# A hybrid decoder layer: the recurrent stage's small products in one run per unit, its distances by ScalarE's bias, the samples' heads gated together

## The chip, the cores and the metric

The kernel is one program on one core of a Trainium2 chip. The metric is device time of one execution in microseconds (us). Before the change three runs took 2379.52, 2382.35 and 2384.54 us, a median of 2382.35 us.

## The reference

One inference step of a hybrid layer for a prompt of 2048 tokens and for 8 samples of 4 tokens: a norm, one input projection, sparse attention (compressed, selected and window keys), a gated linear recurrence with 4 heads, a gated merge of both, an output projection, a last norm. The change is in the recurrence and in when attention's bias tables are loaded. Per head the recurrence is this (`gc` is the log of the forget gate, at most zero):

```python
def step(S, xs):                      # one chunk; S is 128 x 128 per head
    qc, kc, vc, gc = xs
    G = jnp.cumsum(gc, axis=2)
    o_inter = einsum('bhtd,bhde->bhte', qc * exp(G), S)
    D = where(tri, G[:, :, :, None, :] - G[:, :, None, :, :], -inf)
    A = einsum('bhtd,bhtsd,bhsd->bhts', qc, exp(D), kc)
    o = o_inter + einsum('bhts,bhse->bhte', A, vc)
    Gl = G[:, :, -1, :]
    S = exp(Gl)[..., None] * S + einsum('bhsd,bhse->bhde', kc * exp(Gl[:, :, None, :] - G), vc)
    return S, o
...
o = o * rsqrt(mean(o * o, axis=-1, keepdims=True) + EPS)
return o.reshape(B, T, B_WIDTH) * norm_g * silu(zB), S
```

The decay `exp(D)` differs per key channel, so `A` isn't one matrix product.

## The kernel before

The program is written as generators that yield to one another. A projection generator feeds TensorE with 512-column products (line 375, `ps`, weights `wh`/`wl`, inputs `xh`/`xl`). It runs beside the compression of keys, then beside `hgrn()`, the recurrent stage, and then prompt attention follows with the merge. Each `yield` of `hgrn()` grants the projection some 1200 ns worth of products, so these stand between the recurrent steps in TensorE's queue. A framework derives buffers, waits and each engine's order of instructions; every engine takes its queue in that order, and a wait holds what is behind it on the same engine.

`hgrn()` treats 32 units, 8 chunks of 256 tokens by 4 heads. A unit has two halves of 128 tokens (index `j`). Its steps:

- `common()` loads `lf` (log gate), `kt` and `qt`, scans the running sum `G` on VectorE, and makes `Bq`, `Bk` (distances inside groups of 4 tokens), `Xo` (query times `exp(G)`) and `Kd` (key times the decay to the end of the half: a subtraction `E2` on VectorE, line 704, an exponential on ScalarE, a product on GpSimd).
- `factors()` splits the decay between two tokens at the middle of the smallest block that holds both. For each of five levels (64, 32, 16, 8, 4) it makes a tile `X` of `exp(-|G - G at the block's middle|)`: the distance on VectorE (line 732), Abs and Exp on ScalarE (733, 734), keys and queries multiplied in by GpSimd (735, 736). Factors are made two units ahead.
- `scores()` transposes `Kd` (line 743) and multiplies the factors. Each half has a PSUM tile `p4` of its own. Line 755 makes the level-64 product (64 x 64) and two level-32 products (32 x 32); line 759 makes the near ones: levels 16, 8, 4 and `Bk`/`Bq`, each at four diagonal positions of 32 rows and 32 columns of the array. ScalarE copies the far blocks into the score tile `AT` (762, 764). VectorE picks from the four near levels by masks: one product and three `copy_predicated` into `own`, and one into `AT` (766 to 769).
- `values()` makes the state's update (778), the outputs from scores and state (782, 784), the new state (789) and the squares for the norm. After four heads the inverse root follows by three Newton steps (241 to 244), then scale, gate and two stores per head (`gate_scale`, `gate_out`, 658 to 672).
- `sample_heads()` does the samples' 32 tokens, one head at a time, from the seventh unit on, with operands of 32 rows or 32 columns (817, 822, 824, 829, 839, 846), and a norm, a gate and two stores for each head.

The stage starts with its own loads (masks, then `lf`, `kt`, `qt` of the first unit). Ahead of them in the queue of SP, the engine that issues the loads and stores, stand twelve Toeplitz loads of the bias tables (lines 1354 and 1356: `th`, `tl`, `tq`), which prompt attention uses later. Behind the stage, `load_keys` (lines 1397 to 1401) loads the selected keys and values in two parts, t0 = 0 and t0 = 512, while the merge's projection writes its rows by pieces (line 441).

Of the kernel before, what the change touches and what calls it, by code (L numbers as in the profile page):

```python
# [10 lines left out]
F32 = mybir.dt.float32  # L11
# [120 lines left out]
def trunk_kernel(ctx: ExitStack, tc: tile.TileContext, A, O):  # L132
# [100 lines left out]
    def newton_rsqrt(ss, pool):  # L233
# [386 lines left out]
    def hgrn():  # L620
        with ExitStack() as st:
# [6 lines left out]
            lmi = hc.tile([128, 8, 32], I32, name="lmi")  # L628
            ve.tensor_copy(lmi, lm)
            lm3 = hc.tile([128, 32], F32, name="lm3")  # L630
            ve.tensor_copy(lm3, lm[:, 3])
# [17 lines left out]
            def rsqrt(ss):  # L649
                n = ss.shape[0]  # L650
                ve.tensor_scalar(ss, ss, 1.0 / 128, EPS, op0=OP.mult, op1=OP.add)
                y = hp.tile([128, 8], F32, name="rsy", bufs=3)[:n, :ss.shape[1]]
                ve.tensor_scalar(y, newton_rsqrt(ss, hp), sob[:n], None, op0=OP.mult)
                return y

            def gate_scale(o_sb, y, nt, r):

                ve.tensor_tensor(o_sb[:r, :nt], o_sb[:r, :nt], y[:r, :nt, None].to_broadcast([r, nt, 128]), op=OP.mult)

            def gate_out(o_sb, zt, nt, r, h, t0):  # L660
                pt = po.tile([128, 512], F32, name="ov")
                for j in range(nt):
                    pe.transpose(pt[:, j * 128:j * 128 + r], o_sb[:r, j], ident[:r, :r])
                n = (nt - 1) * 128 + r
# [6 lines left out]
                sy.dma_start(obh_d[h * 128:(h + 1) * 128, t0:t0 + n], gh[:, :n])  # L671
                sy.dma_start(obl_d[h * 128:(h + 1) * 128, t0:t0 + n], gl[:, :n])

            def common(h, t0, n, L):
# [3 lines left out]
                def new(name, bufs=2):  # L678
                    return hp.tile([128, n], F32, name=name + sfx, bufs=bufs if n == NC or name == "E" else 1)

                lf = new("lf")
                kt = new("kt", bufs=2)
                qt = new("qt", bufs=2)
# [35 lines left out]
            def factors(c, h):  # L719
# [5 lines left out]
                for li, L in enumerate(LEVELS):  # L725
# [6 lines left out]
                    ve.tensor_tensor(Xv, Gv, ref, op=OP.subtract)  # L732
                    ac.activation(X, X, AF.Abs)
# [6 lines left out]
            def scores(u):  # L740
# [4 lines left out]
                ac.activation(u["kd"], pk[:, :NJ], AF.Copy)  # L745
                u["AT"] = []
                for j in range(NJ):
                    tj = slice(j * 128, (j + 1) * 128)
                    p4 = pa.tile([128, 4, 128], F32, name="p4")

                    near = p4[:, 1].rearrange("p (l t) -> p l t", l=4)
                    for li, L in enumerate(LEVELS[:2]):
                        X = u["Xs"][li][:, tj]
                        for s0 in range(0, 128, 2 * L):
                            mm(p4[s0:s0 + L, 0, s0 + L:s0 + 2 * L], X[:, s0:s0 + L], X[:, s0 + L:s0 + 2 * L], li == 0 or s0 == 64, True)
                    for li, (l, r) in enumerate([(x, x) for x in u["Xs"][2:]] + [(u["Bk"], u["Bq"])]):
                        for b in range(4):
                            bs = slice(j * 128 + 32 * b, j * 128 + 32 * b + 32)
                            mm(near[32 * b:32 * b + 32, li], l[:, bs], r[:, bs], li == 0 and b == 3, True)
# [1323 lines left out]
```

## Time and profile before

| | us |
|---|---|
| median of 3 runs | 2382.35 (2379.52 to 2384.54) |
| profiled execution, its own time | 2394.12 |
| its span (mean granted clock 0.982) | 2392.4 |
| TensorE (PE) busy | 2276.5, 95% |
| VectorE (DVE) busy | 1523.3, 64% |
| ScalarE (ACT) busy | 1180.8, 49% |
| GpSimd (POOL) busy | 1018.8, 43% |

PEld is TensorE's loading of weights, beside its products. A row of a timeline names start, length, engine, line, operation, tiles and count; neighbours of one kind and line are drawn together into one row, so that a row's length covers all of its instructions, and a product's end is modelled: the start of the next is the surer mark. Idle time is put down to the instruction that released the engine, or to "issue" where the profile shows nothing that it waited for. A row by stretch counts busy time of each engine within the two times given.

### The profile page before, as it was taken

To read this page: it belongs to the slowest core of one execution; us is meant where nothing else is said; L and a number is where in the kernel's file an instruction comes from. 1 tells how busy PE (TensorE), PEld (TensorE's weight loads), DVE (VectorE), ACT (ScalarE), POOL (GpSimd) and SP (SyncE) were. 2 spreads that over 40 slices of the span, in tenths; PEclk is the share of its full clock that TensorE was granted. 3 is DMA by queue.
4 is the path that set the end of the run, shared out by engine and by line. 5 is a ranking of instruction groups with operands and counts; after the bars stand their busy time and mean duration, and the time that the engine had idled before them with its cause. 6 is when DMAs were issued, how large, how long until landed. Compare 5 with 4: busy or idle time off the path is not lost.

```text
span 2392.4 us, 56947 instructions
## 1 busy us (share of the span) xinstructions
PE 2276.5 (95%) x22181; PEld 1543.9 (65%) x22181; DVE 1523.3 (64%) x4089; ACT 1180.8 (49%) x2606; POOL 1018.8 (43%) x1184
## 2 busy tenths in 40 slices
PE   6999998999899999999999999899999999999998
PEld 4888775555586556566665556567667666665765
DVE  7555554756632599888753466777677676767543
ACT  5544331531332266666642266356556566667563
POOL 0000102332430065566620045266556576768764
PEclk9999999999999999999999999999999999999999
DMA  6543312677762333443324433322222221211121
GB/s 201 171 142 116 130 72 88 228 250 245 234 161 72 136 133 117 143 128 104 123 87 139 126 113 111 102 62 84 75 77 86 59 69 55 59 47 50 51 59 42
DMA packets 276111, 271.91 MB, mean 114 GB/s; under 512 B 102296, under 2 KB 246176, under 8 KB 268416
## 3 DMA queue, kind: packets, MB, share of 16 engines
q1 hardware_dynamic: 267328, 230.51, 31.5%
q0 software_dynamic: 8512, 37.75, 4.8%
q8 instruction: 174, 2.85, 0.5%
q14 instruction: 97, 0.79, 0.1%
HBM read 184.66 MB, written 87.74 MB: 114 GB/s over the span
## 4 chain that ended last, share of the span: by engine, by line
PE 75%; DVE 9%; DMA 6%; ACT 3%; issue 3%; SPq 2%; POOL 1%; another core or an unknown queue 0%; DVEq 0%; POOLq 0%; ACTq 0%
PE ps L375 19%; PE ps L1847 7%; PE ps L1815 7%; PE ps L456 6%; PE ps L435 5%; PE st L1704 3%; PE st L1694 3%; PE mx L1570 3%; PE ph L1005 2%; PE po L1495 2%; PE po L1498 2%; PE po L1496 2%; PE pt L988 1%; DMA wraw<-in_w_in_dram 1%; PE mx L1572 1%
## 5 line engine op out<-in xcount | busy, mean ns | idle before, releaser
L1489 POOL TENSOR_TENSOR Pl<-P,Ph 128x512 f16<-128x512 f32 x444 | 522.0, 1185 | 355.6 <-ACT Ph L1488 234.6
L1487 ACT ACTIVATE P<-st 128x512 f32<-128x512 f32 x444 | 264.9, 597 | 253.6 <-PE st L1704 199.5
L375 PEld LDWEIGHTS <-wh 128*128 128x128 f16 x2240 | 214.9, 99 | 164.4 <-issue 16.1
L1488 ACT ACTIVATE Ph<-st 128x512 f16<-128x512 f32 x444 | 263.4, 595 | 18.4 <-PE po L1496 11.7
L375 PE MATMUL ps<-xh,wh 128*128 128x512 f16 (+1 forms) x1120 | 234.4, 344 | 6.2 <-DVE row L388 3.5
L375 PE MATMUL ps<-xh,wl 128*128 128x512 f16 (+1 forms) x1120 | 235.3, 345 | 0.0
L375 PE MATMUL ps<-xl,wh 128*128 128x512 f16 (+1 forms) x1120 | 231.8, 342 | 1.2 <-issue 1.2
L1573 DVE TENSOR_REDUCE mps<-mx 128x1 f32<-128x512 f32 (+3 forms) x320 | 186.3, 602 | 55.3 <-PE mx L1570 31.7
L456 PE MATMUL ps<-wh,xh 128*128 128x256 f16 (+1 forms) x680 | 190.9, 281 | 12.3 <-ACT to L464 7.2
L456 PE MATMUL ps<-wh,xl 128*128 128x256 f16 (+1 forms) x680 | 189.9, 280 | 3.9 <-DVE xl L341 3.9
L456 PE MATMUL ps<-wl,xh 128*128 128x256 f16 (+1 forms) x680 | 190.3, 280 | 0.0
L375 PEld LDWEIGHTS <-wl 128*128 128x128 f16 x1120 | 110.2, 100 | 81.1 <-issue 4.4
L1495 PEld LDWEIGHTS <-Ph 128*128 128x128 f16 x1776 | 140.0, 98 | 34.3 <-DVE otmp L1587 3.8
L456 PEld LDWEIGHTS <-xh 128*128 128x128 f16 x1360 | 131.7, 100 | 34.8 <-issue 9.6
L1496 PEld LDWEIGHTS <-Ph 128*128 128x128 f16 x1776 | 128.8, 97 | 32.8 <-issue 0.7
L735 POOL TENSOR_TENSOR X<-X,kt 128x128 f32<-128x128 f32 x160 | 90.6, 566 | 115.2 <-ACT X L734 110.4
L1573 DVE TENSOR_REDUCE mpw<-mx 128x1 f32<-128x512 f32 (+3 forms) x224 | 103.0, 483 | 45.7 <-PE mx L1572 44.0
L1815 PEld LDWEIGHTS <-xh 128*128 128x128 f16 x1280 | 104.5, 98 | 31.6 <-issue 7.8
L1498 PEld LDWEIGHTS <-Pl 128*128 128x128 f16 x1776 | 94.3, 97 | 25.6 <-POOL Pl L1489 7.1
L1495 PE MATMUL po<-vs,Ph 128*128 128x65 f16 x1088 | 105.5, 192 | 2.1 <-DVE otmp L1587 2.0
L1847 PE MATMUL ps<-xh,yh 128*128 128x512 f16 (+1 forms) x272 | 103.0, 379 | 2.3 <-DVE pr L1818 2.3
L1496 PE MATMUL po<-vs,Ph 128*128 128x64 f16 x1088 | 105.1, 193 | 0.0
(529 smaller groups left out, 5740.7 us busy)
## 6 DMA issues: line engine op xcount, KB each, us to landing
wraw<-in_w_in_dram SPq DMA_DIRECT2D x22, 1024.0 KB
xt<-in_x_prompt_dram SPq DMA_DIRECT2D x32, 512.0 KB
ma_d<-row SPq DMA_DIRECT2D x8, 1040.0 KB
out_y_prompt_dram<-xt SPq DMA_DIRECT2D x16, 512.0 KB
sg<-ma_d SPq DMA_DIRECT2D x56, 128.0 KB
sg<-mb_d SPq DMA_DIRECT2D x56, 128.0 KB
q_d<-row SPq DMA_DIRECT2D x4, 1040.0 KB
lf_d<-row SPq DMA_DIRECT2D x4, 1040.0 KB
```

Of the source, the lines that this page charges most:

```text
L375: mm(ps, l[:, kc], xs(r, t0, n)[:, kc], k == 0, k == 23)
L435: mm(ps, l[:, kc, a * 128:(a + 1) * 128], xs(r, t0, n)[:, kc], k == 0, k == 23)
L456: mm(ps, x, w[:, kc], k == 0, k == 23)
L1487: ac.activation(P[:n], ps, AF.Exp, scale=1.0 / QS)
L1488: ac.activation(ph[:n], ps, AF.Exp, scale=1.0 / QS)
L1489: sub.tensor_sub(pl[:n], P[:n], ph[:n])
L1495: mm(po[:, r, :w], ph[:n, rs[r]], v[:n, :w], first and r == 0, False)
L1496: mm(po[:, r, :64], ph[:n, rs[r]], v[:n, w:w + 64], False, False)
L1498: mm(po[:, r, :w], pl[:n, rs[r]], v[:n, :w], False, last)
L1573: ve.tensor_reduce(mp_[:, r, c:c + 1], pmf[:, :n], axis=AX.X, op=OP.max)
L1815: mm(X["ps"], w[:, kc, cs], os_[o][:, kc], k == 0, k == 11)
L1847: mm(X["ps"], X["y"][y][:, kc, i0:i0 + r], W["o", kc // 4][w][:, kc % 4, cs], k == 0, k == 23)
```

## The change

- `newton_rsqrt` becomes `near_rsqrt`: two steps of a higher order in place of three, with the constants folded into the last product.
- The near levels are picked by one product with four 0/1 masks and a sum over the levels, in place of a product and three `copy_predicated`.
- `Kd` and the level-64 distance take no subtraction on VectorE: ScalarE computes `exp(bias - G)` and `|bias - G|` with a per-partition bias, in two calls of 128 columns each.
- The products of a unit go into one `p4` tile for both halves, in one piece of code at raised priority. All use 32 columns of the array: the level-64 product is two products of 32 columns, each with 64 columns moving. The first are those of level 4 (`X4`), then `Bk`/`Bq`.
- `lf`, `kt` and `qt` have three buffers. At the start three more yields stand between the factors of the first and of the second unit.
- The samples' operands are padded with zeros to 128 rows and columns. The outputs of the four heads are collected in `oT`, and there is one transpose, norm, gate and pair of stores for all of them, at the end.
- The Toeplitz loads move to `load_keys`: the four `tq` ahead of the first part, the eight `th`/`tl` behind the second part's keys and ahead of its values.

The diff, cut to its core:

```diff
-        for _ in range(3):
-            ve.tensor_mul(z, y, y)
+        for c in (1.0, 9.0 / 64):
+            ve.scalar_tensor_tensor(z, y, c, y, op0=OP.mult, op1=OP.mult)
             ve.tensor_mul(z, z, ss)
-            ve.tensor_scalar(z, z, -0.5, 1.5, op0=OP.mult, op1=OP.add)
-            ve.tensor_mul(y, y, z)
+            ve.scalar_tensor_tensor(z, z, -10.0 / 3, z, op0=OP.add, op1=OP.mult)
+            ve.scalar_tensor_tensor(y, z, 5.0, y, op0=OP.add, op1=OP.mult)
...
-                lf = new("lf")
-                kt = new("kt", bufs=2)
-                qt = new("qt", bufs=2)
+                lf = new("lf", bufs=3)
+                kt = new("kt", bufs=3)
+                qt = new("qt", bufs=3)
...
-                E2 = new("E", bufs=2)
-                ve.tensor_tensor(E2.rearrange("p (b i) -> p b i", i=L), GL[:, :, L - 1:L].to_broadcast([128, n // L, L]), GL, op=OP.subtract)
                 Kd = new("Kd")
-                ac.activation(Kd, E2, AF.Exp)
+                if n == NC:
+                    for b in range(n // L):
+                        ac.activation(Kd[:, b * L:(b + 1) * L], GL[:, b], AF.Exp, scale=-1.0, bias=GL[:, b, L - 1:L])
...
-                    ve.tensor_tensor(Xv, Gv, ref, op=OP.subtract)
-                    ac.activation(X, X, AF.Abs)
+                    if nb == 2:
+                        for b in range(2):
+                            ac.activation(Xv[:, b], Gv[:, b], AF.Abs, scale=-1.0, bias=Gv[:, b, L - 1:L])
+                    else:
+                        ve.tensor_tensor(Xv, Gv, ref, op=OP.subtract)
+                        ac.activation(X, X, AF.Abs)
...
+                p4 = pa.tile([128, 4, 128], F32, name="p4")
+                first = set()
+                for j in range(NJ):
+                    prod = []
+                    for li, (l, r) in reversed(list(enumerate([(x, x) for x in u["Xs"][2:]] + [(u["Bk"], u["Bq"])]))):
+                        for b in range(4):
+                            bs = slice(j * 128 + 32 * b, j * 128 + 32 * b + 32)
+                            prod.append((b, p4[32 * b:32 * b + 32, 2 * j + 1, 32 * li:32 * li + 32], l[:, bs], r[:, bs]))
+                    prod = prod[4:8] + prod[:4] + prod[8:]
+                    for li, L in enumerate(LEVELS[:2]):
+                        X = u["Xs"][li][:, j * 128:(j + 1) * 128]
+                        for s0 in range(0, 128, 2 * L):
+                            for c0 in range(s0, s0 + L, 32):
+                                prod.append((c0 // 32, p4[c0:c0 + 32, 2 * j, s0 + L:s0 + 2 * L], X[:, c0:c0 + 32], X[:, s0 + L:s0 + 2 * L]))
+                    with tc.high_priority():
+                        for b, o, l, r in prod:
+                            mm(o, l, r, b not in first, True)
+                            first.add(b)
...
-                    ve.tensor_mul(own, near[:, 3], lm3)
-                    for li in range(3):
-                        ve.copy_predicated(own, lmi[:, li], near[:, li])
-                    ve.copy_predicated(AT, lmi[:, 4:], own[:, None, :].to_broadcast([128, 4, 32]))
+                    each = hp.tile([128, 4, 32], F32, name="each")
+                    ve.tensor_mul(each, near, lm4)
+                    ve.tensor_reduce(own, each.rearrange("p l t -> p t l"), axis=AX.X, op=OP.add)
+                    ve.copy_predicated(AT, lmi, own[:, None, :].to_broadcast([128, 4, 32]))
...
-                        for b in range(4):
-                            ve.tensor_scalar(vm[:, b], v, bd[:, 4 * b2 + b:4 * b2 + b + 1], None, op0=OP.mult)
+                        ve.tensor_tensor(vm_[:32], v[:, None].to_broadcast([32, 4, 128]), bd[:, 4 * b2:4 * b2 + 4, None].to_broadcast([32, 4, 128]), op=OP.mult)
...
-                    mm(pb[:32, :32], Bk, Bq, True, True)
+                    mm(pb[:, :32], WIDE["Bk"], Bq, True, True)
...
-                    mm(ov, v, AT, True, False)
+                    mm(ov, v_, AT_, True, False)
...
-                    gate_out(o_sb, load_z(h, 2048, 32), 1, 32, h, 2048)
...
+                pe.transpose(pt[:, :128], oT.rearrange("p h t -> p (h t)"), ident)
...
+                gate_out(o_sb, zt, 1, place)
...
-            for _ in range(3):
+            for _ in range(6):
                 yield
...
+                for g in range(2):
+                    for dl in range(2):
+                        a["TB"][g, dl] = [pc_.tile([128, 4, 128], F16, name=f"t{hl}{g}{dl}") for hl in "hl"]
+                        tq = a["TQ"][g, dl] = pc_.tile([128, 4, 128], F16, name=f"tq{g}{dl}")
+                        sy.dma_start(tq, a["toep"](brh_d, g * 4 * 2 * BRN + BRN + (BRN - 1 - BR0) - 127 - 128 * dl, [[1, 128], [2 * BRN, 4], [1, 128]]))
                 sy.dma_start(a["sel0"], A["c_sel0"].rearrange("p (t j) -> p t j", j=32))
...
+            if t0 > 0:
+                for (g, dl), ts_ in a["TB"].items():
+                    for t_, br in zip(ts_, (brh_d, brl_d)):
+                        sy.dma_start(t_, a["toep"](br, g * 4 * 2 * BRN + BR0 + 128 * dl - 127, [[1, 128], [2 * BRN, 4], [1, 128]]))
```

In TensorE's order before, one half of a unit late in the stage stands like this, behind the transposes of its `Kd` (the size at a row's end is that of the output, with its count; `vs_`, `ATs`, `S0` belong to the samples):

```order
L743 MATMUL pk_14206<-ident_60,Kd_13932 128x128 x2
L755 MATMUL p4_14211<-X0_13939 64x64
L755 MATMUL p4_14211<-X1_13945 32x32 x2
L759 MATMUL p4_14211<-X2_13951 32x32
L822 MATMUL pu_14114<-ATs_13902,vs__13891 128x32
L824 MATMUL pu_14114<-Xo_s_13881,S0_13893 128x4 x8
L759 MATMUL p4_14211<-X2_13951 32x32 x3
L759 MATMUL p4_14211<-X3_13957 32x32 x4
L759 MATMUL p4_14211<-X4_13963 32x32 x4
L759 MATMUL p4_14211<-Bq_13921,Bk_13922 32x32 x4
L375 LDWEIGHTS wh_12587
```

The sample's value product and its eight state products stand in the middle of the half, and projection products (line 375) follow at once. Over the whole program the products of lines 755 and 759 stand in 121 such runs; 2760 projection products of line 375 stand ahead of the first.

After the change the same unit stands in one piece, behind a transpose of another unit's gate (line 663):

```order
L663 MATMUL ov_13843<-ident_60,o_sb_12985 128x128
L777 MATMUL p4_14196<-X4_13969 32x32 x4
L777 MATMUL p4_14196<-Bq_13928,Bk_13929 32x32 x4
L777 MATMUL p4_14196<-X3_13963 32x32 x4
L777 MATMUL p4_14196<-X2_13957 32x32 x4
L777 MATMUL p4_14196<-X0_13945 32x64 x2
L777 MATMUL p4_14196<-X1_13951 32x32 x2
L777 MATMUL p4_14196<-X4_13969 32x32 x4
```

The last row is the first of the second half, whose six rows follow with nothing between them; then come the next gate's transpose and a sample's (`Kd_s`). Over the program these products (line 777) stand in 32 runs, and 2613 projection products are ahead of the first.

In SP's queue before, where attention opens, the second part of the keys (`kas`, `kbs`) and the second part of the values (`vs16`) follow one another, between two writes of projection rows (`mb_d`):

```order
L1401 DMA vs16_16495<-vsx_d_93 128x4x258
L441 DMA mb_d_76<-piece_16538 128x512
L1397 DMA kas0_16491<-ksx_d0_89 64x1536
L1398 DMA kbs0_16492<-ksx_d0_89 128x1536
L1397 DMA kas1_16493<-ksx_d1_90 64x1536
L1398 DMA kbs1_16494<-ksx_d1_90 128x1536
L1401 DMA vs16_16495<-vsx_d_93 128x12x258
L1988 DMA szt_17834<-sz_d_69 128x2x128
L1988 DMA szt_18007<-sz_d_69 128x2x128
L1516 DMA kx1_19305<-kwx_d1_92 128x256
L441 DMA mb_d_76<-piece_16600 128x512
```

The twelve Toeplitz loads stand far ahead of this, in one block before the loads of the recurrent stage. After the change eight of them are at this place:

```order
L1433 DMA kas1_16237<-ksx_d1_90 64x1536
L1434 DMA kbs1_16238<-ksx_d1_90 128x1536
L1440 DMA th00_16240<-brh_d_85 128x4x128
L1440 DMA tl00_16241<-brl_d_86 128x4x128
L1440 DMA th01_16244<-brh_d_85 128x4x128
L1440 DMA tl01_16245<-brl_d_86 128x4x128
L1440 DMA th10_16248<-brh_d_85 128x4x128
L1440 DMA tl10_16249<-brl_d_86 128x4x128
L1440 DMA th11_16252<-brh_d_85 128x4x128
L1440 DMA tl11_16253<-brl_d_86 128x4x128
L1441 DMA vs16_16239<-vsx_d_93 128x12x258
L441 DMA mb_d_76<-piece_16560 128x272
```

They stand behind the keys and ahead of the values and of the next writes of rows. The other four, `tq`, stand ahead of the keys' first part.

## Rows read from the trace of the kernel before

**Rows 1.** The page: busy time by engine, and the chain that ended last.
```profile
PE 2276.5 (95%) x22181; PEld 1543.9 (65%) x22181; DVE 1523.3 (64%) x4089; ACT 1180.8 (49%) x2606; POOL 1018.8 (43%) x1184
...
PE 75%; DVE 9%; DMA 6%; ACT 3%; issue 3%; SPq 2%; POOL 1%; another core or an unknown queue 0%; DVEq 0%; POOLq 0%; ACTq 0%
```

**Rows 2.** By stretch: length, busy us (x instructions) by engine, clock, DMA share, GB/s.
```profile
606.00:720.00 114.00, 102.25 (x949) 81.20 (x948) 56.97 (x122) 45.85 (x114) 43.11 (x60) 0.97 0.71 200
...
836.00:1240.00 404.00, 386.98 (x4187) 245.59 (x4186) 333.13 (x1019) 249.66 (x888) 238.16 (x392) 0.97 0.38 122
...
1300.00:1330.00 30.00, 28.65 (x210) 18.05 (x209) 8.89 (x34) 6.94 (x12) 2.31 (x2) 1.00 0.85 226
```

**Rows 3.** TensorE in order of time: start, us, engine, line, operation, out<-in.
```profile
1043.10 0.48 PE L755 MATMUL p<-X 128*64 128x64 f32 x4
1043.38 0.23 PE L759 MATMUL p<-X 128*32 128x32 f32 x2
...
1043.43 0.34 PE L759 MATMUL p<-X 128*32 128x32 f32 x20
...
1043.63 0.26 PE L759 MATMUL p<-Bq,Bk 128*32 128x32 f32 x7
1043.82 0.61 PE L375 MATMUL ps<-xh,wh 128*128 128x512 f16 x2
...
1048.16 1.46 PE L375 MATMUL ps<-xh,wh 128*128 128x512 f16 x6
1049.55 0.25 PE L817 MATMUL pk<-Bq_s,Bk_s 128*32 128x32 f32 x2
1049.73 0.60 PE L375 MATMUL ps<-xh,wh 128*128 128x512 f16 x2
1050.17 1.89 PE L375 MATMUL ps<-xl,wh 128*128 128x512 f16 x8
1051.90 0.59 PE L375 MATMUL ps<-xh,wl 128*128 128x512 f16 x2
1052.42 0.48 PE L755 MATMUL p<-X 128*64 128x64 f32 x4
...
1052.93 0.44 PE L743 MATMUL pk<-ident,Kd 128*128 128x128 f32 x2
1053.29 0.35 PE L759 MATMUL p<-X 128*32 128x32 f32 x18
...
1053.67 1.47 PE L375 MATMUL ps<-xh,wl 128*128 128x512 f16 x6
```

**Rows 4.** The products' tile: idle time of the engine before them, us, times.
```profile
  issue: 26.2, 85
...
  POOL X L736: 9.4, 6
```

**Rows 5.** Groups of instructions, 606 to 1240: busy us, mean ns, idle before.
```profile
L759 PE MATMUL p<-X 128*32 128x32 f32 x1536 | 38.3, 201 | 0.0
L755 PE MATMUL p<-X 128*32 128x32 f32 (+1 forms) x384 | 35.1, 222 | 4.5 <-POOL X L736 3.4 <-DVE own L768 1.2
...
L759 PE MATMUL p<-Bq,Bk 128*32 128x32 f32 x512 | 20.5, 201 | 0.0
```

**Rows 6.** The same by shape: two of VectorE, two of ScalarE.
```profile
L732 DVE TENSOR_TENSOR X<-G 128x256 f32<-128x256 f32 x160 | 72.2, 494 | 14.0 <-PE p L759 8.3 <-PE p L755 3.7 <-POOL X L736 1.4
...
L394 ACT ACTIVATE row<-ps,neg 128x512 f32<-128x512 f32 x48 | 32.8, 683 | 65.5 <-PE ps L375 65.3
...
L704 DVE TENSOR_TENSOR E<-G 128x256 f32<-128x256 f32 x32 | 18.5, 578 | 0.2
...
L797 ACT ACTIVATE jk<-ov 128x128 bf16<-128x128 f32 x60 | 16.5, 275 | 0.2
```

**Rows 7.** The page, a call of ScalarE with constant scale and bias.
```profile
L1487 ACT ACTIVATE P<-st 128x512 f32<-128x512 f32 x444 | 264.9, 597 | 253.6 <-PE st L1704 199.5
```

**Rows 8.** One line of Toeplitz loads: ns of an issue, min/median/max.
```profile
L1356 SPq DMA_DIRECT2D tq<-brh_d x4: 506/508/702, 607.8 to 614.3; - x4
```

More of the change, by code (lines that the diff above doesn't have):

```diff
@@ L627, in hgrn @@
             sy.dma_start(lm, A["c_lmask"].rearrange("p (l t) -> p l t", l=8))
[L628 to L631, printed above, removed]
+            lmi = hc.tile([128, 4, 32], I32, name="lmi")
+            ve.tensor_copy(lmi, lm[:, 4:])
+            lm4 = hc.tile([128, 4, 32], F32, name="lm4")
+            ve.tensor_copy(lm4, lm[:, :4])
             ATs = []
@@ L670, in gate_out @@
                 ve.tensor_sub(gl[:, :n], g[:, :n], gh[:, :n])
-                sy.dma_start(obh_d[h * 128:(h + 1) * 128, t0:t0 + n], gh[:, :n])
-                sy.dma_start(obl_d[h * 128:(h + 1) * 128, t0:t0 + n], gl[:, :n])
+                for d, x in ((obh_d, gh), (obl_d, gl)):
+                    to, x = place(d, x)
+                    sy.dma_start(to, x)
+            WIDE = {}
             def common(h, t0, n, L):
@@ L746, in scores @@
                 u["AT"] = []
                 for j in range(NJ):
[L748 to L755, printed above, removed]
@@ L802, in sample_heads, with zeros @@
             def sample_heads():
+                def zeros(name, shape):
+                    t_ = hc.tile([128] + shape, F32, name=name)
+                    gp.memset(t_, 0.0)
+                    return t_
+                for nm in ("Bk", "Kd"):
+                    WIDE[nm] = zeros(nm + "_s", [128])
+                v_, AT_, kd_, vm_ = zeros("vs_", [128]), zeros("ATs", [32]), zeros("kd_s", [128]), zeros("vm", [4, 128])
+                oT = hc.tile([128, 4, 32], F32, name="oT")
                 for h in range(4):
                     G, qt, kt, Bq, Bk, Xo, Kd, eG = common(h, 2048, 32, 4)
-                    v = hp.tile([32, 128], F32, name="vs_")
+                    v = v_[:32]
                     sy.dma_start(v, ib_d[2048:2080, h * 128:(h + 1) * 128])
@@ L808, in sample_heads @@
                     sy.dma_start(S0, A["state_hgrn"][0, :, h].rearrange("b d e -> d b e"))
-                    vm = hp.tile([32, 4, 128], F32, name="vm", bufs=1)
                     def masked(b2):
-                        for b in range(4):
-                            ve.tensor_scalar(vm[:, b], v, bd[:, 4 * b2 + b:4 * b2 + b + 1], None, op0=OP.mult)
+                        ve.tensor_tensor(vm_[:32], v[:, None].to_broadcast([32, 4, 128]), bd[:, 4 * b2:4 * b2 + 4, None].to_broadcast([32, 4, 128]), op=OP.mult)
@@ L840, in sample_heads @@
-                    kd = hp.tile([32, 128], F32, name="kd_s", bufs=1)
+                    pe.transpose(pk[:, 0], WIDE["Kd"], ident)
+                    kd = kd_[:32]
                     ve.tensor_copy(kd, pk[:32, 0])
@@ L854, in sample_heads, with place @@
                     sy.dma_start(O["s_hgrn"][0, :, h].rearrange("b d e -> d b e"), Sn)
+                    yield
+                pt = po.tile([128, 512], F32, name="pk")
+                pe.transpose(pt[:, :128], oT.rearrange("p h t -> p (h t)"), ident)
+                o_sb = hp.tile([128, NJ, 128], F32, name="o_sb", bufs=5)[:, :1]
+                ss = hp.tile([128, 4 * NJ], F32, name="ss")[:, :1]
+                ac.activation(o_sb[:, 0], pt[:, :128], AF.Copy)
+                jk = hp.tile([128, 128], BF, name="jk", bufs=1)
+                ac.activation(jk, pt[:, :128], AF.Square, accum_out=ss)
+                zt = hp.tile([128, NC], F32, name="zt", bufs=6)
+                def place(d, x):
+                    return d[:, 2048:2080].rearrange("(h p) t -> p h t", p=128), x[:, :128].rearrange("p (h t) -> p h t", t=32)
+                sy.dma_start(*place(zb_d, zt)[::-1])
+                yield
+                gate_scale(o_sb, rsqrt(ss), 1)
+                yield
+                gate_out(o_sb, zt, 1, place)
             beside = sample_heads()
```

60 lines of the change are left out of this document (23 added, 37 removed).

## The prediction

> **What bounds the kernel now.** I read the shares of the page first, then the table by stretch, then one stretch of TensorE in order of time, then the lines and the tile of the products that the change rewrites. The page has TensorE busy for 2276.5 of 2392.4 us and on 75% of the chain that ended last [rows 1]: a microsecond saved elsewhere counts only where TensorE waits for it. The recurrent work itself lies between 836 and 1240 us (a few units are pulled ahead into 606 to 720). There TensorE is busy 387 of 404 us, VectorE 333, ScalarE 250, GpSimd 238 [rows 2]. TensorE is the bound, VectorE at 82% is second. TensorE is never short of work, since projection products stand between the recurrent steps; it loses time only where the next instruction of its queue isn't ready, and inside small products. So the question is how long the small products hold TensorE.
>
> **The small products.** One unit (256 tokens of a head) has two halves of 128 tokens. Undisturbed, a half runs from 1043.10 to 1043.82, 0.72 us [rows 3]. Of that the first four instructions (the 64-wide product and one 32-wide, each issued twice, since its operands are f32) take from 1043.10 to 1043.38, 0.28 us, and the other 34 with what follows take 0.44 us. At 1052.42 the same half is broken into by two transposes and takes until 1053.67, 1.25 us. The two transposes have 128 columns each, some 0.11 us an issue and two issues, 0.22 us; so the break costs 1.25 - 0.72 - 0.22 = 0.31 us. A lone narrow product gives the same price without any other work: the six products before it start at 1048.16 and take 1.73/8 = 0.216 us each, so they are through at 1049.45, and the next wide product starts at 1049.73. That is 0.28 us for two instructions of 32 columns [rows 3]. TensorE pays about 0.28 us each time it goes from wide products to narrow ones and back. The tile view agrees: 85 times, 26.2 us in all, 0.31 us each, the engine stood idle before one of these products with nothing to wait for ("issue") [rows 4].
>
> What the change does to them: (a) In TensorE's order the products of the 32 units stand in 121 separate runs before and in 32 after, one per unit. 89 runs less at 0.28 us are 25 us. (b) The 64-wide product becomes two 32-wide ones with 64 columns each, which go to two different column groups. Within the narrow part 34 instructions pass in 0.44 - 0.17 us (0.17 is the step back to a wide product: the end of the lone one, 1049.55 to 1049.73, less its own few ns), so 8 ns each; with twice the columns and only two groups to share I take 27 ns for each of the four instructions that replace the two. The wide product's 0.28 - 2 x 0.008 = 0.26 us become 0.11 us, 64 times: 10 us. Together **-35 us**. From the other side: a unit after the change is 72 instructions at 8 ns, 8 at 27 ns and one step in and out, 0.58 + 0.22 + 0.28 = 1.08 us, 34.6 us for 32 units. The three groups are busy 38.3 + 35.1 + 20.5 = 93.9 us now [rows 5], which counts waits and the modelled ends too: at most 59 us are gained. If all units were undisturbed now (1.44 us + 0.1 us of entry), it is 32 x 0.46 = 15 us. I take 35, which lies nearest to the two priced rows, and keep 15 and 59.
>
> A rule of the Trainium skill speaks against (b). TensorE: Matmul & The Clock Gate (Part 1, on the floors of small matmuls) has start-to-start never below about 25 ns however few the columns. By it, 80 instructions would hold TensorE 2.0 us a unit, an estimate from that page, and the sum would be some 39 us worse. The trace shows the opposite: from 1043.38 to 1043.82 there are 34 starts, 13 ns each with the step out counted [rows 3]; by that rule, the rows do not agree.
>
> **The samples' heads.** Their products use 32 rows or 32 columns of the array now and the full array after, with operands padded by zeros. 28 such calls go (per head: one score, one value product, two transposes, two updates, one output transpose); at 0.28 us each at most 8 us. Some stand beside one another already, so I take half, 4 us, and 1 us for the six transposes that are left out: **-5 us** (0 to -9).
>
> **VectorE, ScalarE, GpSimd.** VectorE loses 32 subtractions at 494 ns and 32 at 578 ns, 34 us [rows 6], besides shorter root and mask steps. ScalarE gets two 128-column calls with a [128,1] bias in place of one of 256 columns, twice a unit. A 128-column call takes 275 ns [rows 6]; a per-partition operand costs 683 - 597 = 86 ns on 512 columns [rows 6, 7]; so 2 x 361 - 406 = 0.32 us, 64 times, 20 us. ScalarE goes from 250 to 270 us, VectorE from 333 to under 299 (the masks and roots come off as well), in a stage of some 365 us. Neither passes TensorE, so both edits count **0** on the path; what hides ScalarE's 20 us is TensorE's busy row [rows 2]. Bounds: -10 us (the products wait 9.4 us for GpSimd's factors now [rows 4], which could vanish) and +20 us (all of ScalarE's increase on the path).
>
> **The moved loads.** Twelve Toeplitz loads leave the front of the stage, where TensorE is idle 114 - 102.3 = 11.8 us [rows 2], and go behind the stage. Each holds SP's queue some 0.5 to 0.6 us [rows 8], 7 us in all. At the front the stage's own loads start sooner, but the first run of products also moves ahead of some 150 projection products in TensorE's order, so the cushion shrinks by what the loads gain: **0** (-10 to +5). Behind the stage they stand in SP's queue before the second part of the values and before the write of the next projection piece; that piece's buffer is what ScalarE, and so TensorE's projections, wait for. The transfers run into 1300 to 1330, where the DMA engines are already 85% busy and TensorE idles 1.35 us [rows 2]: **+4 us** (0 to +15).
>
> **New waits.** TensorE runs its queue in order. With 10% less of its own work in the stage, each recurrent result has that much less cover, and a run of products at raised priority stands directly behind GpSimd's last factor: **+5 us** (0 to +25).
>
> **Sum.** -35 - 5 + 0 + 0 + 4 + 5 = -31 us. Against the profiled execution (2394.12 us, a span of 2392.4) that is 2363. The median of the three runs, 2382.35, is 11.8 us lower; so I forecast 2351 us.
>
> **Rivals.**
> 1. *More than the sum.* The waits at these products go too (10 us), the front stalls less (10 us) and the moved loads are free: -35 - 5 - 10 - 10 + 5 = -55, 2327 us. For it: VectorE gets a tenth more room. Against: a shorter stage makes waits, it doesn't take them. 2334 as a middle; chance 0.18.
> 2. *The cushion is eaten.* The unit's run waits for GpSimd about 0.6 us each time, 27 x 0.6 = 16 us: 2367 us. For it: one run per unit means that no part can start early, and the fourth and fifth factors are the last that GpSimd makes. Against: it waited only 9.4 us in all for them before [rows 4]. Chance 0.21.
> 3. *The narrow products don't overlap better than now.* If the 80 instructions of a unit pass at the mean rate of a whole half, 0.72/38 = 19 ns, a unit takes 80 x 0.019 + 0.28 = 1.80 us instead of 1.08: 23 us are lost, 2374 us. Against it are the 13 ns of the narrow part alone [rows 3]. The floor of the Trainium skill, named above, would be a stronger form of it, 2390 us. Chance 0.04.
> 4. *Slower.* ScalarE feeds GpSimd, GpSimd feeds the run, and ScalarE's two extra calls per level and decay lengthen that chain. If each of 27 steady units waits over 31/27 = 1.15 us more than in the sum, the gain is gone; at 2 us it is -31 + 54 = +23, 2405 us. For it: the row by stretch has GpSimd fed, not saturated [rows 2], so it follows ScalarE. Against: two units of factors are kept ahead. Chance 0.07.
> 5. *No change*: what the stage gains is lost in the opening of attention (+15) and in waits (+16): 2382 us. Chance 0.05.
>
> The forecast has the remaining 0.45 (2340 to 2360). What a measurement here can tell from no change is about 0.2%, 4.8 us. Faster takes the forecast and rivals 1 to 3: 0.88; same 0.05; slower 0.07. The range that leaves out 2 in 10: from 2327 (rival 1 in full) to 2378 (rival 2 with the moved loads at their worst).
>
> **What would show it.** Right: the products of a unit pass in about 1.1 us from first to next wide product; their groups fall from 93.9 us to under 50; "issue" idle before them falls from 26 us to under 10; the end of the last recurrent unit comes some 30 us earlier and the rest of the run keeps its length. Wrong: TensorE idle before these products "until GpSimd" of over 25 us (rivals 2, 4); runs of over 1.6 us without a wait (rival 3); ScalarE above 85% between the first and last unit; TensorE idle over 10 us where attention opens, with SP or a DMA named.

## The result and the profile after

The changed kernel took 2350.04 us (2343.77 to 2355.1, 4 runs), against 2382.95 of the kernel before beside it: a ratio of 0.9861, interval 0.9838 to 0.9884. Forecast were 2351 us. In a second group the same kernel had a ratio of 0.9854 (0.9826 to 0.9883).

The profiled execution took 2343.77 us, 50 less than the profiled one of before. Of these, 23.3 us lie ahead of the recurrent stage: the samples' attention ends at 581.1 instead of 604.4 us. Other kernels below that have the Toeplitz loads in front, as before, end it at 587 to 604 us, so much of this belongs to the execution and not to the change. What compares best is the stretch from the last product of the samples' attention to the merge's first product. Its row in the table by stretch, first of before, then of after (length; busy us of TensorE, its weight loads, VectorE, ScalarE, GpSimd, each with instructions; clock; DMA share; GB/s):

```profile
604.40:1524.40 920.00, 872.26 (x8244) 561.52 (x8243) 591.83 (x1703) 447.88 (x1260) 367.14 (x550) 0.98 0.42 128
```
```profile
581.10:1473.60 892.50, 837.16 (x8386) 551.72 (x8384) 564.78 (x1377) 458.08 (x1310) 357.50 (x553) 0.98 0.44 133
```

The stretch is 27.5 us shorter. TensorE is busy 35.1 us less and idle 920.0 - 872.3 = 47.7 us before, 55.3 after: the work went, and 7.6 us of it came back as waits. The two stretches don't hold quite the same work: with the loads moved, 44 more products of line 375 stand in it (2075 against 2031; 35 of them have 272 columns and start 0.116 us apart, 9 have 512 and start 0.216 us apart) and 24 fewer of attention's, some 4 us more by an estimate from these starts. So on equal work the gain is about 32 us, close to the 33 of the medians. Busy time and chain of the whole page, the answer to [rows 1]:

```profile
PE 2228.3 (95%) x22303; PEld 1525.9 (65%) x22303; DVE 1498.8 (64%) x3780; ACT 1191.0 (51%) x2658; POOL 1009.2 (43%) x1190
...
PE 56%; DVE 9%; DMA 4%; ACT 3%; issue 2%; SPq 1%; POOL 0%; ACTq 0%; POOLq 0%; DVEq 0%
```

The chain of after could be followed back only to 557 us, so its shares add up to 75% of the span, and its 56% for TensorE can't be set against the 75% of before.

A unit's products in order of time, which answer to [rows 3] (L777 is the new line of all of them):

```profile
851.98 0.27 PE L777 MATMUL p<-X 128*32 128x32 f32 x8 [0.98 <-POOL X L749]
852.07 0.25 PE L777 MATMUL p<-Bq,Bk 128*32 128x32 f32 x8
852.13 0.51 PE L777 MATMUL p<-X 128*32 128x32 f32 x31
...
852.53 0.49 PE L777 MATMUL p<-X 128*32 128x32 f32 x23
852.95 0.52 PE L375 MATMUL ps<-xl,wh 128*128 128x272 f16 x3
```

From 851.98 to 852.95, 0.97 us for 80 instructions and both halves; 27 of the 32 units take this; four hold a wait, and one, from 636.27 us on, took 1.64 us while the granted clock was 0.50. The forecast was 1.08 us; before, two undisturbed halves took 1.44. The idle time before the products' tile, against [rows 4]:

```profile
  POOL X L749: 19.0, 11
...
  issue: 4.4, 16
```

"Issue" fell from 26.2 to 4.4 us; the wait for GpSimd's factors doubled. This answer adds up the idle time of the products and of their weight loads (PEld): all of the "issue" is the weight loads', and of the wait for GpSimd the products' own part is 8.7 us, where before it was 3.4 of 9.4. TensorE's waits from 815 to 1190 us (line, releaser: us, times, longest) show what else it waited for:

```profile
PE ov L804 <- DVE zt L666: 6.7, 5, 2.7
PE pu L800 <- issue: 6.5, 4, 2.4
PE ps L375 <- DVE row L397: 3.9, 3, 2.6
PE ov L663 <- DVE o_sb L658: 3.6, 3, 1.9
```

Three of the four end with VectorE. The two subtractions that left it are now ScalarE's L743 and L711, at 391 and 395 ns, where I had taken 361:

```profile
L743 ACT ACTIVATE X<-G 128x128 f32<-128x128 f32 x64 | 22.3, 391 | 9.5 <-DVE G L694 4.4 <-DVE ss L651 4.0 <-DVE rsq L238 1.0
L711 ACT ACTIVATE Kd<-G 128x128 f32<-128x128 f32 x64 | 22.1, 395 | 4.8 <-DVE mxs L208 2.2 <-DVE G L694 1.8 <-PE pk L756 0.3
```

The Trainium skill (ScalarE: Activation LUTs, What ACT_TABLE_LOAD costs) gives 280 ns and 0.833 ns an element for a call with such a bias, which makes an estimate of 387 ns for 128 elements; these rows agree, with 391 and 395.

### The profile page after: what moved, and what is told of

It reads as the page before. It is cut to its first block, busy times and chain, and to the rows that moved or that the text cites. A ratio compares the mean times of both kernels' runs of the same rounds, so it can differ in the third digit from the quotient of the medians.

```text
span 2342.0 us, 56775 instructions
## 1 busy us (share of the span) xinstructions
PE 2228.3 (95%) x22303; PEld 1525.9 (65%) x22303; DVE 1498.8 (64%) x3780; ACT 1191.0 (51%) x2658; POOL 1009.2 (43%) x1190
## 4 chain that ended last, share of the span: by engine, by line
PE 56%; DVE 9%; DMA 4%; ACT 3%; issue 2%; SPq 1%; POOL 0%; ACTq 0%; POOLq 0%; DVEq 0%
PE ps L375 10%; PE ps L1887 7%; PE ps L1855 7%; PE ps L435 5%; PE st L1744 3%; PE mx L1610 3%; PE st L1734 3%; PE ps L456 3%; PE po L1535 2%; PE po L1538 2%; PE po L1536 2%; DVE X L745 1%; PE mx L1612 1%; PE st L1740 1%; PE st L1741 1%
## 5 line engine op out<-in xcount | busy, mean ns | idle before, releaser
L1529 POOL TENSOR_TENSOR Pl<-P,Ph 128x512 f16<-128x512 f32 x444 | 521.6, 1184 | 327.2 <-ACT Ph L1528 185.5
L375 PEld LDWEIGHTS <-wh 128*128 128x128 f16 x2240 | 218.6, 99 | 172.7 <-issue 20.5
L375 PE MATMUL ps<-xh,wl 128*128 128x512 f16 (+1 forms) x1120 | 230.1, 341 | 0.0
L706 POOL TENSOR_TENSOR Xo<-Xo,qt 128x256 f32<-128x256 f32 x32 | 31.7, 990 | 278.8 <-ACT Xo L705 278.8
L1734 PE MATMUL st<-qb,kbs 128*128 128x512 f16 x272 | 103.1, 379 | 1.7 <-ACT Ph L1528 1.5
```

Source lines behind the costliest of these rows:

```text
L375: mm(ps, l[:, kc], xs(r, t0, n)[:, kc], k == 0, k == 23)
L1529: sub.tensor_sub(pl[:n], P[:n], ph[:n])
L1734: mm(ps, kb, flat(u["b"]), True, False)
```

## The experiments

Times are ratios to the kernel before in the same group, since its own median moved between groups (2382, 2394, 2382 us).

**e1, the products alone.** The code of the diff for `p4`, one tile for both halves, put into the kernel before:

```diff
-                    p4 = pa.tile([128, 4, 128], F32, name="p4")
+                p4 = pa.tile([128, 4, 128], F32, name="p4")
...
+                    with tc.high_priority():
+                        for b, o, l, r in prod:
```

> The kernel before with the products' part alone: one PSUM tile for both halves, the level-64 product in two pieces of 32 columns, all products of a unit in one raised piece; VectorE, ScalarE, GpSimd, the loads and the samples' heads as before. Theory (the products carry the gain by themselves): a unit's 80 instructions hold TensorE about 1.0 us from the first to the next wide product, and the kernel takes 2383 - 35 + 5 = 2353 us, 2346 to 2360. Rival (the gain needs the relief of VectorE as well, since the one run waits for the last factor): TensorE stands idle over 15 us before these products until GpSimd, and the time is 2368 us or more.

Measured: 1.0034 (1.0022 to 1.0046), 2389 us: 0.3% slower. The products pass as in the kernel after (0.97 us a unit where undisturbed), and TensorE is busy less, yet the stretch is longer:

```profile
589.00:1522.20 933.20, 856.42 (x8373) 552.35 (x8371) 612.11 (x1701) 446.40 (x1260) 366.79 (x549) 0.96 0.42 126
...
PE ov L663 <- DVE o_sb L658: 12.2, 4, 5.2
PE ps L375 <- DVE row L397: 8.9, 4, 3.4
PE mx L1644 <- DVE repp L1640: 8.1, 3, 4.8
PE p L762 <- POOL X L736: 5.7, 4, 2.6
```

Busy 15.8 us less, idle 76.8 against 47.7. My theory falls, and the rival has the direction but not the place: the products wait 5.7 us for GpSimd, and the large waits end with VectorE, at the scaling of the gate (L658) and at the projection's own rows (L397). And the granted clock is 0.96. VectorE itself is busy 20.3 us longer than before (612.1 against 591.8 us) with as many instructions (1701 against 1703). Its subtractions of line 732 alone grew from 72.2 to 86.5 us; each takes 594 ns on the mean where [rows 6] had 494:

```profile
L732 DVE TENSOR_TENSOR X<-G 128x256 f32<-128x256 f32 x160 | 86.5, 594 | 0.9 <-PE p L762 0.9
```

In e1's trace 82 of these subtractions had GpSimd busy beside them for over nine tenths of their time, and took 704 ns on the mean; 38 had it busy for under a tenth, and took 412. In the trace of before 45 took 584 and 82 took 413. That GpSimd is the cause is not shown by a run. One of the waits, and the 12 us behind it:

```profile
1053.40:1058.60 5.20, 0.03 (x1) 0.00 (x0) 4.89 (x19) 0.30 (x1) 3.20 (x7) 0.88 0.11 32
1058.60:1064.00 5.40, 5.38 (x16) 2.79 (x17) 2.08 (x6) 0.69 (x2) 0.00 (x0) 0.50 0.16 49
1064.00:1070.00 6.00, 6.00 (x41) 4.12 (x39) 2.28 (x7) 2.80 (x14) 1.12 (x1) 0.98 0.07 22
```

While TensorE stood idle for 5.2 us, VectorE was busy for 4.89. Then TensorE ran 5.4 us at 0.50, 1.2 GHz: a wait of 5.2 us cost about 2.7 us more behind it.

**e2, the moved loads alone.**

```diff
-                    sy.dma_start(t_, toep(br, o, [[1, 128], [2 * BRN, 4], [1, 128]]))
...
+            if t0 > 0:
+                for (g, dl), ts_ in a["TB"].items():
```

> The kernel before with the twelve Toeplitz loads moved behind the stage, and nothing else. Theory (nothing in front, +4 behind): 2387 us, 2381 to 2393, and TensorE's idle time between the end of the stage's projection and the first 200 us of attention is 2 to 8 us more than before. Rival (the front of the stage gains what its own loads gain): 2373 us, with TensorE idle under 4 us between the end of the samples' attention and the first recurrent products. Second rival (the transfers and issues are hidden at both places): 2383 us, within 4.

Measured: 1.0004 (0.9987 to 1.002). Neither the 4 us nor a gain can be told from nothing. The first recurrent loads went out at 583 us, 1 us after the samples' attention; in e3, with the Toeplitz loads in front, at 602, 15 us after it. But the first state update started at 644.5 there and at 639.3 in e3: in these two profiles an earlier start bought nothing.

**e3, the samples' heads alone.**

```diff
-                    mm(pb[:32, :32], Bk, Bq, True, True)
+                    mm(pb[:, :32], WIDE["Bk"], Bq, True, True)
```

> The kernel before with the samples' heads alone changed: operands padded to 128, one transpose, norm, gate and pair of stores for the four heads at the end. Theory: 28 fewer changes between narrow and full-size products, half of them worth 0.28 us, and six transposes less: -5 us, 2378 us, 2373 to 2383. Rival (these products already stood beside other narrow ones, or wait anyway): 2383 us, within 3.

Measured: 0.9971 (0.9957 to 0.9985), 7 us less. The time is as the theory had it; of its reason little is seen. TensorE is busy as long as before in the stretch (872.25 against 872.26 us), at a mean clock of 0.972 against 0.976 by the traces' records, so at most some 3 us of its work went. It is idle 4.2 us less, while VectorE is busy 11 us less, for the edit also leaves it one norm and one gate in place of four:

```profile
586.90:1502.70 915.80, 872.25 (x8238) 563.88 (x8237) 580.77 (x1622) 445.65 (x1248) 371.25 (x556) 0.97 0.42 129
```

That VectorE's relief made the gain is a rival that no run sets apart.

**e4, VectorE's and ScalarE's edits alone** (bias, masked sum, two-step root; `each` and `own` with one buffer for want of room).

```diff
-                    ve.tensor_tensor(Xv, Gv, ref, op=OP.subtract)
+                            ac.activation(Xv[:, b], Gv[:, b], AF.Abs, scale=-1.0, bias=Gv[:, b, L - 1:L])
```

> The kernel before with VectorE's and ScalarE's edits alone: Kd and the level-64 distance by ScalarE's bias, the levels picked by a masked sum, the two-step inverse root. Theory (both engines lie beside TensorE): VectorE is busy some 35 us less and ScalarE some 20 us more in the stage, and the time stays: 2383 us, within 4. Rival (the products' waits for factors vanish): 2373 us, and the idle time before the products until GpSimd falls from 9.4 us to under 2. Second rival (ScalarE's longer chain to GpSimd's last factor): 2393 us or more, with that idle time over 15 us.

Measured: 1.0027 (1.0014 to 1.004), 6 us more, between theory and second rival. VectorE's busy time falls from 591.8 to 556.6 us, ScalarE's grows by 18.5:

```profile
590.10:1512.30 922.20, 877.23 (x8244) 565.58 (x8243) 556.61 (x1463) 466.39 (x1324) 362.14 (x550) 0.97 0.42 128
```

By themselves these edits gain nothing, as long as TensorE is the bound. Why they cost 6 us stays open: TensorE is idle 45.0 us in the stretch, less than before, and the single buffers, which the change doesn't have, were not tested apart.

**e5, both: e1's and e4's edits together.**

> The kernel before with two parts of the change: the products in one run, and VectorE's and ScalarE's edits (bias, masked sum, two-step root). The products alone took 2389 us and the engines' edits alone 2386, against 2382. Theory (VectorE is the second bound: with TensorE's part shorter, TensorE waits for VectorE's rows, gates and states, and only both edits together free it): clearly under 2382, 2350 to 2368 us, with TensorE idle under 22 us between 836 and 1240, against 31 with the products alone. Rival (the parts add): 2394 us, 2387 to 2400. Second rival (the gain hangs on the samples' heads, the third buffers or the longer opening): 2375 to 2386.

Measured: 0.9957 (0.9942 to 0.9972), 10 us less, where the two single results add up to 15 more. So they don't add, and the theory has the direction; but 10 us is less than its 14 to 32, the interval just touches the second rival, and between 836 and 1240 us TensorE is idle 28.8 us, not under 22. Over the stretch it is idle 910.9 - 846.1 = 64.8 us, 12 less than in e1 (the single buffers of e4 are in this kernel too):

```profile
599.10:1510.00 910.90, 846.06 (x8372) 550.70 (x8371) 573.05 (x1463) 461.81 (x1324) 358.93 (x550) 0.97 0.42 129
```

**e6, after with the subtractions on VectorE again.**

```diff
-                            ac.activation(Xv[:, b], Gv[:, b], AF.Abs, scale=-1.0, bias=Gv[:, b, L - 1:L])
+                    ve.tensor_tensor(Xv, Gv, ref, op=OP.subtract)
```

> The kernel after with the subtractions on VectorE put back: Kd and the level-64 distance as before, all else as after. Theory (VectorE's relief by 34 us is what lets the products' gain through): 2350 + 10 to 25 us, so 2360 to 2375, with TensorE's idle time in the stage up by as much, before steps that VectorE feeds. Rival (ScalarE has no room either, and the edit does nothing): 2350, within 5. Second rival (ScalarE's longer chain cost time): under 2345.

Measured: 0.9926 (0.9909 to 0.9944), 16 us above the kernel after. That one was not run beside e6 to e8; its stretch, 892.5 us against 907.4 here, says the same. The theory stands in time and place: TensorE is idle 63.6 us in the stretch (55.3 in after), and the row that VectorE owes it is the largest wait. The idle time makes 8.2 us of the difference; the other 6.7 are busy time, at a mean clock of 0.97 against 0.98:

```profile
596.40:1503.80 907.40, 843.85 (x8386) 554.03 (x8383) 587.49 (x1439) 448.15 (x1246) 365.15 (x553) 0.97 0.43 131
...
PE ps L375 <- DVE row L397: 9.2, 5, 3.6
```

**e7, after without the raised priority.**

```diff
-                    with tc.high_priority():
-                        for b, o, l, r in prod:
+                    for b, o, l, r in prod:
```

> The kernel after with the products at ordinary priority: same tile, same 32-column products, same code, but in TensorE's order they stand in 103 runs in place of 32. Theory (each entry into narrow products costs 0.28 us): 71 x 0.28 = 20 us more, 2370 us, 2362 to 2378. Rival (a run that may start in parts waits less for GpSimd's last factor, which pays for the entries): 2350, within 5. Second rival (entries among other work cost next to nothing, the gain came from shorter instructions): 2350 as well, but with runs of under 0.28 us for their share and the same idle time before the products.

Measured: 0.989 (0.9869 to 0.991), 7 us above the kernel after, with intervals that overlap: between the theory's 12 to 28 and the rival's 5. An entry has its price: "issue" before these products, the weight loads' again, is 22.4 us in 76 waits against 4.4 in 16, 0.30 us for each one more. TensorE is busy 22.5 us longer in the stretch than in after, a part of it for the clock (0.97 against 0.98). The first rival's saving is there as well: TensorE is idle 12.6 us less, and the wait for GpSimd before the tile fell from 19.0 to 1.4 us.

```profile
  issue: 22.4, 76
...
  POOL X L749: 1.4, 6
```

**e8, after with the loads back in front; e10, after with two buffers only.** The tiles of the loads and the third buffers don't fit together, so e8 has both edits (`kt` and `qt` as `lf`).

```diff
-                lf = new("lf", bufs=3)
+                lf = new("lf", bufs=2)
```

> The kernel after with the Toeplitz loads back in front of the stage; since their tiles take the room, lf, kt and qt have two buffers again. Theory (the loads cost 4 us behind the stage and nothing in front; the third buffers do nothing): 2346 us, 2342 to 2351. Rival (the loads in front delay the stage's first unit, and two buffers make SP's loads wait): 2360 us or more.

> The kernel after with two buffers for lf, kt and qt, the Toeplitz loads staying behind the stage. With the loads back and two buffers the ratio was 0.992. Theory (it is the buffers: with two of each a unit's loads wait for the readers of the unit before last, and the moved loads matter only since they make the room): 0.990 to 0.994. Rival (it was the loads in front of the stage): 0.986, within 0.002. Second rival (that ratio was another chip's state): 0.986 here and for the kernel after alike, with no difference between them of over 0.002.

Measured: e8 0.9919 (0.9899 to 0.9938), e10 0.9886 (0.9866 to 0.9907), the kernel after beside e10 0.9854. e8's theory falls and its rival holds; e10 lies between its theory and the first rival. Two buffers cost some 8 us, and with the loads in front it is 15, but e8 is of another group, and the 8 us between e8 and e10 lie within their intervals. The intervals of e10, e11 and e12 touch that of the kernel after, but all of their times lie above its own beside them (2353.24 us and more, against 2341.86 to 2352.59). In e10's trace TensorE is idle no longer than in after (903.2 - 847.3 = 55.9 us); its waits fall elsewhere. The mean clock over the stretch is 0.966 against 0.979 by the trace's records, some 11 us, as much as the 10.7 by which the stretch is longer. All four executions agree: their granted clocks are 0.982 to 0.985, those of the kernel after beside them 0.985 to 0.989, some 8 us of the whole on the mean. So the price of two buffers came as clock and not as idle time; what the third buffers do to the waits stays open.

```profile
581.80:1485.00 903.20, 847.28 (x8389) 557.66 (x8387) 557.63 (x1382) 458.51 (x1310) 358.59 (x554) 0.97 0.43 131
```

**e9, after once more** (no edit).

> The kernel after once more, unchanged, so that the others of this group have it beside them on the same chip. Expected: a ratio of 0.986 to before, within 0.003, and 890 to 900 us from the last transpose of the samples' attention to the merge's first product.

Measured: 0.9854, and 893.2 us for the stretch. As expected.

**e11, after with the level-64 product in one piece.**

```diff
-                            for c0 in range(s0, s0 + L, 32):
-                                prod.append((c0 // 32, p4[c0:c0 + 32, 2 * j, s0 + L:s0 + 2 * L], X[:, c0:c0 + 32], X[:, s0 + L:s0 + 2 * L]))
+                            prod.append((s0 // 32, p4[s0:s0 + L, 2 * j, s0 + L:s0 + 2 * L], X[:, s0:s0 + L], X[:, s0 + L:s0 + 2 * L]))
```

> The kernel after with the level-64 product as one product of 64 columns again, inside the same single run per unit. Theory (a 64-column product takes 0.26 us and two of 32 columns 0.11): a unit's run takes 0.97 + 2 x 0.15 = 1.27 us undisturbed, and the time is 2350 + 10 us, a ratio 0.004 above the kernel after's. Rival (the 0.26 us was the entry into narrow products, paid once per run anyway): a run of 1.0 us and the same ratio as after, within 0.002.

Measured: 0.99 (0.9879 to 0.9921), 11 us above the kernel after. The theory stands in direction and time, but the run is longer than it said:

```profile
852.91 0.27 PE L776 MATMUL p<-X 128*32 128x32 f32 x8
853.00 0.25 PE L776 MATMUL p<-Bq,Bk 128*32 128x32 f32 x8
853.06 0.79 PE L776 MATMUL p<-X 128*32 128x32 f32 x28
...
853.75 0.79 PE L776 MATMUL p<-X 128*32 128x32 f32 x21
854.46 0.41 PE L375 MATMUL ps<-xl,wh 128*128 128x272 f16 x2
```

From 852.91 to 854.46 are 1.55 us for 76 instructions, against 0.97 for 80. Each of its two 64-column products costs 0.29 us more than the two narrow ones in its place, and the run is no shorter than two separate halves were before (1.44). Single starts around the first of them are 853.17 for the last narrow product, 853.30 and 853.41 for its own two issues, and 853.56 for the next narrow one. Of these 0.38 us 0.11 lie between the two issues; the rest I put down to going to another width and back, from 32 columns to 64, as from full width to 32. No run parts this from the time that the wide product itself takes.

**e12, after with the gate's transposes in `p4`.**

```diff
-                pt = po.tile([128, 512], F32, name="ov")
+                pt = pa.tile([128, 4, 128], F32, name="p4").rearrange("p a b -> p (a b)")
```

> The kernel after with the gate's transposes in the products' PSUM tiles (p4, two buffers) in place of the values' single one (ov), for which TensorE waits 6.7 us before the values, until VectorE has read the gate's transposes. Theory: these waits and some of the 3.6 us before the transposes go, 2350 - 7 us, a ratio 0.003 under the kernel after's. Rival (the wait moves to the products' run, which then waits for VectorE's read of the gate): the same ratio or up to 0.004 above, with idle time before the products until VectorE.

Measured: 0.9889 (0.9867 to 0.9911), 8 us above. The wait before the values went, and others came, the three largest of them for VectorE. The rival's ratio came (0.0035 above); the place is another, the gate's own transposes (L663) and the projection's rows. Over the stretch TensorE is idle 56.7 us against 55.3, so the waits account for little of the 8 us. The kernel after stays the fastest of these.

```profile
PE ps L375 <- DVE row L397: 7.9, 6, 3.2
...
PE p L663 <- DVE zt L666: 4.1, 2, 3.0
PE ov L806 <- DVE S L811: 3.3, 2, 2.2
```

## Why the prediction was right, and where not

- *The products, -35.* Right in size: TensorE's busy time fell by 35.1 us, where products and heads together were to give 40. The busy time of the products' tile alone, with all three groups taken as one, of before and of after:

```profile
604.40:1524.40 920.00, 64.94 (x2432) 46.84 (x2432) 41.69 (x256) 30.25 (x192) 0.98 0.42 128
```
```profile
581.10:1473.60 892.50, 34.20 (x2560) 30.50 (x2560) 18.04 (x64) 30.10 (x192) 0.98 0.44 133
```

  After are the 34 us that the sum had. But 93.9 us before counted the same time in two or three of the groups, so the most that these rows allowed was some 30 us, not 59; and the 26.2 us of "issue", read as idle time of the engine, are the weight loads'. The split was off. The 64-wide product was worth 32 x 0.58 = 18.6 us of TensorE's time (e11, busy 17.9 us longer than after), not 10; some 17 to 20 us are left for the number of runs and the heads, not 30. An entry does have its price (e7: 0.30 us), but the 64-wide product is such a change of width itself, and I had priced it as one long instruction. The Trainium skill (TensorEngine Tiling (Array Packing), Key Properties) says that a change of tiling mode drains TensorE; e7 and e11 agree, with 0.30 and 0.29 us a change.
- *The Trainium skill's floor of 25 ns between starts* (TensorE: Matmul & The Clock Gate, Part 1), which I set aside: 80 starts in 0.97 us are 12 ns each, entry counted. It doesn't bind here.
- *The heads, -5.* Right in size: -7 alone. Of the reason given, fewer changes of width, e3's trace shows some 3 us at most.
- *VectorE and ScalarE, 0.* This step failed. It said that neither passes TensorE and that TensorE's busy row hides the edits. Alone they cost 6 us; in the changed kernel ScalarE's bias is worth 16 (e6); and without these edits the products gain nothing at all (e1). VectorE's 82% of the stage was close enough to a bound that in e1 the shortening of TensorE turned into waits for it. The share by itself doesn't tell: it is 81% after (299.2 of 368.3 us, 815.7 to 1184) and 85% in e6 (315.6 of 370, 840 to 1210). I took a saving on TensorE as safe and VectorE's as worthless; each needs the other. The masked sum saves next to nothing; the relief is the two subtractions. Of before (a group's busy time, and the tile view's min/median/max), then of after:

```profile
L768 DVE COPY_PREDICATED own<-lmi,p 128x32 f32<-128x32 int32 x192 | 31.4, 184 | 1.5
...
L766 DVE TENSOR_TENSOR own<-p,lm x64: 159/178/193, 655.2 to 1233.3; 128x32 f32<-128x32 f32 x64
```
```profile
L745 DVE TENSOR_TENSOR X<-G 128x256 f32<-128x256 f32 x128 | 70.2, 594 | 0.0
...
L790 DVE TENSOR_REDUCE own<-each 128x32 f32<-128x128 f32 x64 | 23.8, 372 | 3.8 <-issue 2.6
...
L789 DVE TENSOR_TENSOR each<-p,lm 128x128 f32<-128x128 f32 x64 | 18.0, 282 | 3.9 <-ACT AT L786 3.6
```

  31.4 + 64 x 0.178 = 42.8 us became 41.8. Of the subtractions, 72.2 + 18.5 us [rows 6] became 70.2, which is 20.5 less and not the 34 of the sum: the 128 that are left take 594 ns each, as in e1, not 494.
- *The moved loads, +4.* Not told from 0 (e2). The first half of it, that an earlier start in front buys nothing, is what one profile each of e2 and e3 shows. The third buffers, for which the loads make room and which I gave no term, are worth some 8 us (e10).
- *New waits, +5.* Right: idle time in the stretch grew by 7.6 us, 5.3 of it the products' own wait for GpSimd, 3.4 to 8.7 us (6.6 of it at once).
- *Signs that I named.* "Issue" under 10 us and 1.1 us a unit came. The products' groups under 50 us did not: they are busy for 70.5 us after, because every product counts with its modelled length of about 0.2 us, and where the groups overlap the same time counts in two or three of them. The starts, or the tile's 34.2 us, were the mark to read. And the last unit did not come 30 us earlier. The values' product, first and last start, of before and of after:

```profile
L782 PE MATMUL ov<-v,AT x128: 272/275/377, 840.8 to 1249.7; 128*128 128x128 f32 x128
```
```profile
L804 PE MATMUL ov<-v,AT x128: 272/276/378, 821.0 to 1226.9; 128*128 128x128 f32 x128
```

  That is 645.3 and 645.8 us after the end of the samples' attention: the recurrent units took as long as before, while TensorE did more of the projections between these points (3075 products against 2899), and the gain shows only behind the stage.

So the time was right, and the account behind it was right for TensorE alone. Costed one by one, the parts measure +8, +1, -7 and +6 us, +8 together; the whole is -33. That rests on their coming together, which the prediction did not see; so far its right time was luck. The -10 of e5, the -7 of e3 and the 8 us of the third buffers make 25 of the 33; the other 8 no run has set apart, and the longer opening (three more yields) had no run of its own.

## What to carry to other kernels

When the bound engine is to be relieved, look at the second engine in the same stage: at 82% here, a tenth off the first by itself turned into waits for the second, and an edit that is worth nothing by itself can decide whether the other one pays. Count the changes of width in a stream of small products, not the products. Read a saving from the busy time and the idle time of a stretch that starts and ends with the same instructions, count what stands between them, and don't read it from the groups' busy time when products overlap.

## What the runs showed of the hardware

Narrow products of 32 columns started 12 ns apart over a whole unit, and going to another width and back cost some 0.3 us (0.28 in [rows 3], 0.29 in e11, 0.30 in e7). A wait of TensorE can cost more than itself: behind the idle 5.2 us at 1053 us of e1 the granted clock was 0.50 for 5.4 us. Over the stretch e1 had a mean clock of 0.958 against 0.976 of before, by the traces' records, some 17 us of its 933. Without that its busy time would be 33 us under the kernel before's; so the waits took 29 us by their length and 17 by the clock behind them. VectorE's subtraction of 128x256 took 412 to 415 ns on the mean where GpSimd was busy beside it for under a tenth of its time, and 584 (before), 704 (e1) and 745 ns (after) where it was for over nine tenths.
